# Moving ten of nineteen adaLN chunks of a two-layer trunk from TensorE matmuls to VectorE dot products

## The chip, the cores and the metric

The kernel runs on 1 core of one Trainium2 chip. The metric is the device time of one execution in microseconds (us). The time before is 1082.05 us, the median of 3 runs (1081.66 to 1082.13).

## The reference

Two layers work on 256 tokens of width 1024 in f32. Each layer first forms six modulation vectors of 1024 numbers from one conditioning vector (adaLN), then runs three attention branches between one input projection and one output projection, then a mixture of 16 experts.

```python
c_act = jax.nn.silu(c)
for layer in range(DEPTH):
    mod = jnp.dot(c_act, w_mod[layer]) + b_mod[layer]
    sh1, sc1, g1, sh2, sc2, g2 = jnp.split(mod[:, None, :], 6, axis=-1)
    u = rms_norm(x, norm1_g[layer]) * (1.0 + sc1) + sh1
    x = x + g1 * token_mixers(u, ...)      # w_in, 3 branches, gates, w_out
    u = rms_norm(x, norm2_g[layer]) * (1.0 + sc2) + sh2
    x = x + g2 * grouped_moe(u, ...)
return rms_norm(x, final_g)
```

What matters here is `mod`: a vector of 1024 times a 1024 x 6144 matrix, 24 MB of weights a layer, for a result of 6144 numbers.

## The kernel before

Tokens and channels stand on the 128 partitions. The program of each engine is one fixed order, written out by hand (`tc.manual_schedule()`); engines meet through semaphores.

**Stages.** The prologue is followed by the mixers of layer 0 (to about 320 us), its experts (to about 545 us), the mixers of layer 1 (to about 830 us) and its experts. A mixer is a list of 24 steps, two (`h` = 0, 1) for each of the twelve column groups in `ORDER`. A step multiplies the normalised tokens by one 1 MB block of `w_in` (48 or 24 matmuls), and `step_done` then runs, in the order of `INNER = 'FVTS'`, what is due: follow-ups, the values, the turn (transposes) and the scores of the attention jobs. The nine jobs start at steps 12 to 20 (`JOBS`). After the list come the branch projections, two gate projections `gA0` and `gA1` with the branch A in between, and the output projection.

**Splitting.** f32 weights are cut in two parts before TensorE reads them: `prep_one` casts half a block on ScalarE (line 279, high part) and subtracts it on VectorE (line 280, low part); `split_to` lets this run two halves ahead (`AHEAD`). Four buffers hold the halves.

**A job.** `act("S", step)` calls `scores` (line 692, TensorE), `softmax` (maxima on VectorE, lines 748 to 755; exponentials on ScalarE, line 758) and `normalise` (reciprocals on VectorE, line 767, which need the sums that the exponentials leave).

**The adaLN chunks.** A layer has 12 chunks of 512 numbers. `mod_matmul` (line 423) makes one with two 1 MB blocks and matmuls that use 32 columns of the array each; `mod_copy` (line 430, ScalarE) takes it out of PSUM; one step later `mod_finish` turns it with four transposes (line 437), reduces it on VectorE (line 439) and adds the bias (line 460, sometimes also 463). `MOD_PLAN` says at which step which (layer, chunk) is made: 13 chunks in the mixers of layer 0 (eight of its own, five of layer 1) and 6 in those of layer 1; `EDGE` puts one more between the experts of layer 0. The first four chunks of layer 0 are made otherwise, by `mod_rows` (line 450): the same weights, transposed, stand as rows of 1024 numbers, and one VectorE instruction multiplies such a block of 128 rows with the conditioning vector (`crow`) and adds up each row. A chunk is four blocks, in two units of `modt`.

**The stream.** All weights come through one list (`self.stream`, `plan`), issued by `pump` on the SP queue in that order, one DMA of 1 MB a unit, as soon as a slot is free: `raw0` to `raw5` (`RAW_BUFS`), and at times `x0` to `x4`, `h0` to `h3`, `uh`, `ul`, `gb`. A slot is freed when its reader is done, and the release pumps. The experts read 96 blocks of 1 MB in each layer through the same list; in the middle of them stands a branch that would do the experts' overflow (`rest`, line 1544) and isn't taken, and that TensorE, ScalarE and VectorE each pass.

Of the kernel before, what the change touches and what calls it, by code (L numbers as in the profile page):

```python
# [10 lines left out]
F32 = mybir.dt.float32  # L11
# [13 lines left out]
L = 2  # L25
D = 1024
T = 256
# [59 lines left out]
ONCES = ["gb"]  # L87

ORDER = ['gB0', 'gB1', 'bi', 'bq', 'cq', 'ck', 'cv', 'aq', 'ak', 'gC0', 'av', 'gC1']
RAW_BUFS = 6  # L90
LATE = ["x0", "x1", "x2"]
HALVES = ["h0", "h1", "h2", "h3"]
NEAR = 8


MOD_PLAN = [{5: (0, 4), 6: (0, 5), 7: (0, 6), 9: (0, 7), 11: (0, 8), 13: (0, 9), 14: (0, 10), 15: (0, 11), 17: (1, 0), 18: (1, 1), 19: (1, 2), 21: (1, 3), 22: (1, 4)}, {3: (1, 6), 5: (1, 7), 7: (1, 11), 8: (1, 10), 9: (1, 9), 14: (1, 8)}]
EDGE = {0: (1, 5)}
EDGE_AT = 7

# [51 lines left out]


class Unit:
    __slots__ = ("src", "n", "key", "tile", "slot", "halves", "block", "halved", "rows", "rest", "layer", "wide", "once")

    def __init__(self, key, src, n=512, block=None):
        self.key, self.src, self.n, self.block = key, src, n, block
        self.tile, self.slot, self.halves, self.halved = None, None, None, False
        self.rows, self.rest, self.layer, self.wide = False, None, 0, True
        self.once = False  # L160


class Kernel:
    def __init__(self, ctx, tc, a):
# [5 lines left out]
        self.stream, self.issued = [], 0  # L170
        self.slots = [f"raw{i}" for i in range(RAW_BUFS)]
        self.parts = list(HALVES)
# [21 lines left out]
    def t(self, pool, shape, dt, tag, bufs=1):  # L194
        return pool.tile(shape, dt, tag=tag, name=self.nm(tag), bufs=bufs)
# [9 lines left out]
    def pump(self):  # L205
        while self.issued < len(self.stream):
            u = self.stream[self.issued]
            if u.block is not None and u.block not in self.ready:
                return
            if u.rest is not None:  # L210
                self.load(u.rest, u.rest.src(), 1)
                self.issued += 1
                continue
            fits = [x for x in self.slots if u.layer <= self.l or x[0] == "r"]
            if u.once:
                fits = self.once + fits
            if not fits:
                return
            u.slot = fits[0]
            (self.once if u.slot in self.once else self.slots).remove(u.slot)  # L220
            if u.slot in ONCE:
                pool = {"gb": self.e}.get(u.slot, self.ring)
                u.tile = self.t(pool, [128, 4, 512], F32, u.slot, ONCE[u.slot])
            else:
                pool = {"uh": self.g, "ul": self.g}.get(u.slot, self.ring)
                u.tile = self.t(pool, [128, 4, 512], F32, u.slot)
            src = u.src()
            if u.rows:
                for b in range(2):
                    self.nc.sync.dma_start(u.tile[:, 2 * b:2 * b + 2], src[:, b])  # L230
            elif u.halved:
                for h in range(2 if u.halved == 2 else 1):
                    self.load(u, src, h)
            else:
                self.nc.sync.dma_start(u.tile[:, :, :u.n], src)
            self.issued += 1
# [104 lines left out]

    def cact_row(self):

        self.crow = self.t(self.w, [128, 2, 4, T], F32, "y")[:, 0].rearrange("p a b -> p (a b)")
        self.nc.sync.dma_start(self.crow[0:1], self.a["crow"])

    def fill_row(self):
# [336 lines left out]
    def scores(self, qt, q, blocks, k, kblock):  # L684

        nc = self.nc
        nk = 256 if qt else 128
        s = [self.psum("y") for _ in range(2)]
        for j, b in enumerate(blocks):
            for r in range(2):  # L690
                rows = slice(64 * r, 64 * r + 64)
                nc.tensor.matmul(s[r][:, nk * j:nk * j + nk], q[rows, b, 128 * qt:128 * qt + 128],
                                 k[rows, kblock(b), 0:nk], start=True, stop=True)
        return s
# [185 lines left out]
    def mixers(self, l, parts, angles):  # L880
        nc, a = self.nc, self.a
# [63 lines left out]
        state = {}  # L945

        jobs = {}

        def job(br, qt, blocks, s0):
            jobs[s0] = br, qt, blocks  # L950

        def scores(br, qt, blocks):
            q = {"A": lambda: self.qA, "B": lambda: self.qB, "C": lambda: self.qC}[br]()
            k = {"A": lambda: self.kA, "B": lambda: self.qkB, "C": lambda: self.kC}[br]()
            s = self.scores(qt, q, blocks, k, (lambda b: 0) if br == "B" else (lambda b: b))
            return self.softmax(br, qt, blocks, s)

        def act(what, step):
            if what == "F":
                for fn in after.get(step, ()):  # L960
                    fn()
            elif what == "V" and step - 3 in jobs:
                self.values(*jobs[step - 3], state.pop(step - 3))
            elif what == "T" and step - 2 in jobs:
                state[step - 2] = self.turn(jobs[step - 2][0], state[step - 2])
            elif what == "S" and step in jobs:
                state[step] = self.normalise(*jobs[step], *scores(*jobs[step]))

        def load_bias():
            self.bias = t(self.ring, [128, 8, T], F32, LATE[0])  # L970
# [27 lines left out]

        mods = MOD_PLAN[l]

# [8 lines left out]
        def step_done(step, c, h):  # L1009
            if h == 1:  # L1010
                post(c)
            for what in INNER:
                act(what, step)
            if step - 1 in mods:
                self.mod_finish(*mods[step - 1], held.pop("mod"))
            if step in mods:
                held["mod"] = self.mod_copy(self.mod_matmul(*mods[step]))
# [51 lines left out]
        self.router_shift()  # L1069
        for c in ("gA0", "gA1"):  # L1070
            outs = [self.psum("mm") for _ in range(2)]
            for _ in self.by_channel(("in", l, c), outs, *self.u_parts()):
                pass
            if c == "gA1":
                self.slots += ["uh", "ul"]
                self.pump()
            if c == "gA0":
                self.sg["A"] = t(w, [128, KT, T], F32, "sg", 2)
            for d in range(2):
                k = 4 * int(c[2]) + 2 * d  # L1080
                nc.scalar.activation(self.sg["A"][:, k:k + 2], outs[d].rearrange("p (e t) -> p e t", e=2), AF.Sigmoid)
            if c == "gA0":
                self.mh = [t(w, [128, 4, T], F32R, "q", 2) for _ in range(2)]
                self.ml = [t(w, [128, 4, T], F32R, "p", 2) for _ in range(2)]
            else:
                self.table(AF.Sqrt)
            self.branch("A", int(c[2]), False, True)
# [9 lines left out]
        for oc in range(2):  # L1097
            outs = [self.psum("mm") for _ in range(2)]
# [517 lines left out]
    def plan(self):  # L1616

        a = self.a

        def block(name, l, c, h, n=512):  # L1620

            o = sum(COLS[x][1] for x in list(COLS)[:list(COLS).index(c)]) * D if isinstance(c, str) else 1024 * 512 * c
            o += 512 * n * h
            return lambda: a[name][l, o:o + 512 * n].rearrange("(p k n) -> p k n", p=128, k=4)

        def mod(l, c):
            for h in range(2):
                self.add(("mod", l, c, h), block("w_mod", l, c, h), split=False)

        def rows(l, i):  # L1630
            u = self.add(("modt", l, i), lambda: a["w_modt"][l, 2 * i:2 * i + 2].rearrange("b p (a k) -> p b a k", a=2),
                         split=False)
            u.rows = True
            return u

        def fill(l, s):
            if s in MOD_PLAN[l]:
                mod(*MOD_PLAN[l][s])

        def proj(l, c):  # L1640
            n = COLS[c][1]
            for h in range(2):
                self.add(("in", l, c, h), block("w_in", l, c, h, n), n)

        for l in range(L):
            order = list(enumerate(half_order(l)))
            first = len(self.stream)
            if l == 0:
                for s in range(4):
                    rows(0, s).halved = 2  # L1650
                    rows(0, 4 + s).halved = 2
                    for i, c in enumerate(ORDER[:N_SPLIT]):
                        n = COLS[c][1]
                        key = ("in", l, c, s // 2)
                        if s % 2 == 0:
                            u = Unit(key, block("w_in", l, c, s // 2, n), n)
                            u.halved = 1
                            self.stream.append(u)
                        else:
                            u = Unit(("rest", *key), None)  # L1660
                            u.rest = next(x for x in self.stream if x.key == key)
                            self.stream.append(u)
                            u = u.rest
# [5 lines left out]
            for s, (c, h) in order:  # L1669
                n = COLS[c][1]  # L1670
                u = self.add(("in", l, c, h), block("w_in", l, c, h, n), n, split=l == 0 or s >= 2 * N_EDGE)
# [8 lines left out]
                    self.add(("br", l, br.upper(), c), block("w_branch_" + br, l, 0, c))  # L1680
            for c in range(2):
                proj(l, f"gA{c}")
                self.add(("br", l, "A", c), block("w_branch_a", l, 0, c))
            for oc in range(2):
                for h in range(2):
# [14 lines left out]
            for u in self.stream[-2:]:  # L1700
                u.halved, u.wide = 1, False
                r = Unit(("rest", *u.key), None)
# [116 lines left out]
```

## Time and profile before

| what | us |
|---|---|
| median of 3 runs | 1082.05 |
| the profiled execution | 1081.17 |
| its span | 1079.6 |
| TensorE busy in the span | 1040.0 |
| VectorE busy | 553.1 |
| ScalarE busy | 394.4 |
| bytes by DMA | 336.58 MB, mean 312 GB/s |

The span runs from the first to the last instruction; the execution is 1.6 us longer than its span. Busy time of TensorE counts modelled ends of pipelined matmuls, so the distance from one matmul's start to the next says more of its pace than a duration.

### The profile page before, as it was taken

The numbers are of one execution on the slowest core, as the hardware profiler recorded it, in microseconds if no ns is written. First come the engines' busy times: TensorE is split into PE (matmuls) and PEld (weight loads), VectorE is DVE, ScalarE is ACT, GpSimd is POOL, SyncE is SP. The second block draws the span as 40 slices with busy tenths as digits, with TensorE's granted clock in tenths as the row PEclk, the third lists the DMA queues.
The fourth block names the chain that finished last, engine by engine and source line by source line (L and its number), as shares of the span: only waits on it lengthen the run. The fifth ranks groups of instructions, "written<-read, shape, count | busy, mean of one in ns | idle before, by whom it ended". The sixth has DMA issues, their size and how long they took to land. (4 is left out here: it accounts for less than half of the span.)

```text
span 1079.6 us, 19208 instructions
## 1 busy us (share of the span) xinstructions
PE 1040.0 (96%) x7750; PEld 707.6 (66%) x7750; DVE 553.1 (51%) x1333; ACT 394.4 (37%) x746; POOL 1.5 (0%) x11
## 2 busy tenths in 40 slices
PE   7899999999999999999999999999998999979996
PEld 5778777799975444444388787779997534325344
DVE  6967767556643232222265687776664323222224
ACT  4445456664531111111144446777453211001021
POOL 0000000000000000000000000000000000000000
PEclk9999999999999999999999999999999999999997
DMA  9997776597676999999977966246765699999991
GB/s 348 341 360 305 301 290 239 216 369 269 234 304 227 383 420 420 418 420 421 407 284 284 345 259 234 80 157 245 266 236 229 250 390 420 421 418 419 421 381 39
DMA packets 53846, 336.58 MB, mean 312 GB/s; under 512 B 5617, under 2 KB 11889, under 8 KB 15474
## 3 DMA queue, kind: packets, MB, share of 16 engines
q1 hardware_dynamic: 53746, 335.25, 79.1%
q8 instruction: 63, 1.03, 0.4%
q14 instruction: 37, 0.30, 0.1%
HBM read 334.18 MB, written 1.05 MB: 311 GB/s over the span
## 5 line engine op out<-in xcount | busy, mean ns | idle before, releaser
L280 DVE TENSOR_TENSOR h<-raw,h 128x1024 fp32r<-128x1024 f32 (+1 forms) x130 | 152.5, 1214 | 59.7 <-ACT h L279 59.7
L1447 PE MATMUL mm<-raw,gb 128*32 128x512 f32 (+1 forms) x656 | 171.1, 596 | 1.2 <-DMA raw<-in_exp_w_dram 1.2
L612 PE MATMUL mm<-uh,h 128*128 128x256 f32 x480 | 138.7, 289 | 4.6 <-ACT h L279 4.6
L615 PE MATMUL mm<-uh,h 128*128 128x256 f32 x480 | 137.0, 285 | 2.7 <-DVE h L280 2.7
L614 PE MATMUL mm<-ul,h 128*128 128x256 f32 x480 | 136.3, 284 | 0.0
L279 ACT CAST h<-raw 128x1024 fp32r<-128x1024 f32 (+1 forms) x130 | 129.1, 1042 | 17.3 <-PE mm L869 7.2
L1527 DVE TENSOR_TENSOR x<-y,x 128x512 fp32r<-128x512 f32 (+1 forms) x34 | 22.5, 660 | 158.5 <-ACT x L1526 158.5
L612 PEld LDWEIGHTS mm<-uh,h 128*128 128x128 f32 x480 | 91.7, 191 | 14.5 <-issue 7.9
L1447 PE MATMUL mm<-x,gb 128*32 128x512 f32 (+1 forms) x312 | 94.5, 595 | 0.0
L615 PEld LDWEIGHTS mm<-uh,h 128*128 128x128 f32 x480 | 91.7, 191 | 3.8 <-DVE h L280 3.8
L614 PEld LDWEIGHTS mm<-ul,h 128*128 128x128 f32 x480 | 91.8, 191 | 0.0
L1413 DVE SCALAR_TENSOR_TENSOR xT<-y,mod,xT 128x256 f32<-128x256 f32 x128 | 53.3, 477 | 73.7 <-PE y L1538 73.7
L1447 PE MATMUL mm<-h,gb 128*32 128x512 f32 (+1 forms) x496 | 83.5, 595 | 0.0
L1447 PE MATMUL y<-raw,gt 128*32 128x512 f32 (+1 forms) x224 | 74.9, 594 | 0.0
L593 PE MATMUL mm<-h,uh 128*128 128x512 f32 (+1 forms) x176 | 71.1, 404 | 0.0
L595 PE MATMUL mm<-h,ul 128*128 128x512 f32 (+1 forms) x176 | 69.1, 393 | 0.0
L594 PE MATMUL mm<-h,uh 128*128 128x512 f32 (+1 forms) x176 | 69.0, 392 | 0.0
L1447 PEld LDWEIGHTS mm<-raw,gb 128*32 128x32 f32 (+1 forms) x656 | 44.1, 117 | 31.3 <-issue 26.6
L1357 ACT ACTIVATE gb<-y,mod,sc 128x256 f32<-128x256 f32 (+1 forms) x40 | 20.9, 522 | 100.0 <-DVE gb L1359 100.0
L1421 ACT COPY gt<-t 128x512 f32<-128x512 f32 x16 | 9.4, 586 | 128.0 <-PE t L1420 128.0
L1447 PE MATMUL y<-h,gt 128*32 128x512 f32 (+2 forms) x312 | 53.8, 572 | 1.4 <-ACT gt L1421 1.4
L1447 PEld LDWEIGHTS mm<-x,gb 128*32 128x32 f32 (+1 forms) x312 | 25.1, 122 | 43.3 <-issue 39.5
(319 smaller groups left out, 2059.5 us busy)
## 6 DMA issues: line engine op xcount, KB each, us to landing
raw<-in_exp_w_dram SPq DMA_DIRECT2D x78, 1024.0 KB, 14.8
raw<-in_w_in_dram SPq DMA_DIRECT2D x48, 1024.0 KB, 7.0
x<-in_exp_w_dram SPq DMA_DIRECT2D x45, 1024.0 KB, 15.5
h<-in_exp_w_dram SPq DMA_DIRECT2D x41, 1024.0 KB, 16.8
raw<-in_w_mod_dram SPq DMA_DIRECT2D x37, 1024.0 KB, 7.3
ul<-in_exp_w_dram SPq DMA_DIRECT2D x13, 1024.0 KB, 14.2
uh<-in_exp_w_dram SPq DMA_DIRECT2D x9, 1024.0 KB, 17.7
raw<-in_w_modt_dram SPq DMA_DIRECT2D x16, 512.0 KB, 7.3
```

Source lines behind the costliest of these rows:

```text
L279: nc.scalar.copy(hi[:, :, :u.n], src)
L280: nc.vector.tensor_sub(lo[:, :, :u.n], src, hi[:, :, :u.n].bitcast(F32))
L593: nc.tensor.matmul(o, uh, hi[:, k, :u.n], start=(kk == 0), stop=False)
L594: nc.tensor.matmul(o, uh, lo[:, k, :u.n], start=False, stop=False)
L595: nc.tensor.matmul(o, ul, hi[:, k, :u.n], start=False, stop=(kk == 7))
L612: nc.tensor.matmul(o, hi[:, k, cs], mh[kk], start=(kk == 0 and b % 2 == 0), stop=False, skip_group_check=True)
L614: nc.tensor.matmul(o, hi[:, k, cs], ml[kk], start=False, stop=False, skip_group_check=True)
L615: nc.tensor.matmul(o, lo[:, k, cs], mh[kk], start=False, stop=(kk == 7), skip_group_check=True)
L1357: self.nc.scalar.activation(out, src, AF.Identity, bias=shift, scale=scale)
L1413: nc.vector.scalar_tensor_tensor(self.xT[:, k + b], ps[:, T * b:T * b + T], self.mod[l][:, 5, k + b:k + b + 1], self.xT[:, k + b], op0=ALU ...
L1447: self.nc.tensor.matmul(o[c:c + step], lhs[:, c:c + step], x, start=start, stop=stop, skip_group_check=True)
L1527: self.nc.vector.tensor_sub(yl, ps, yh.bitcast(F32))
```

## The change

Five of the 13 chunks in the mixers of layer 0 and five of the 6 in those of layer 1 are no longer matmuls but `mod_rows`. In each layer three of them (six units, twelve blocks) stand in the attention steps 12 to 20, one or two blocks a step as `ROWS_IN` says, between `softmax` and `normalise`; the other two (four units of two blocks) stand in the loops over `gA0` and `gA1`, one unit after each `h`. The remaining matmul chunks move to other steps. A unit of `modt` is now stored with its two blocks side by side (8 KB a partition) and loaded by one DMA; the first eight units keep two DMAs of 512 KB. There are seven `raw` slots in place of six; `crow` has a place of its own for the whole kernel (before, it lay in a tile that the mixers wrote later), and the buffer `dynamic_dma_scratch_size` is set to 4 KB.

```diff
-RAW_BUFS = 6
+RAW_BUFS = 7
-MOD_PLAN = [{5: (0, 4), 6: (0, 5), 7: (0, 6), 9: (0, 7), 11: (0, 8), 13: (0, 9), 14: (0, 10), 15: (0, 11), 17: (1, 0), 18: (1, 1), 19: (1, 2), 21: (1, 3), 22: (1, 4)}, {3: (1, 6), 5: (1, 7), 7: (1, 11), 8: (1, 10), 9: (1, 9), 14: (1, 8)}]
+MOD_PLAN = [{5: (0, 7), 8: (0, 8), 11: (0, 9), 14: (0, 10), 16: (0, 11), 18: (1, 2), 20: (1, 3), 22: (1, 4)}, {9: (1, 9)}]
+ROWS_PLAN = [[(0, i) for i in range(8, 14)], [(1, i) for i in range(12, 18)]]
+ROWS_AT = (11, 12, 14, 15, 17, 18)
+ROWS_IN = {12: 1, 13: 1, 14: 2, 15: 1, 16: 1, 17: 2, 18: 1, 19: 1, 20: 2}
+ROWS_LATE = [[(1, i) for i in range(4)], [(1, i) for i in range(20, 24)]]
...
-        self.crow = self.t(self.w, [128, 2, 4, T], F32, "y")[:, 0].rearrange("p a b -> p (a b)")
+        self.crow = self.t(self.g, [128, D], F32, "crow")
...
+        blocks = iter([(i, b) for i in ROWS_PLAN[l] for b in range(2)])
...
             elif what == "S" and step in jobs:
-                state[step] = self.normalise(*jobs[step], *scores(*jobs[step]))
+                parts = scores(*jobs[step])
+                for _ in range(ROWS_IN[step]):
+                    i, b = next(blocks)
+                    self.mod_rows(*i, (b,))
+                state[step] = self.normalise(*jobs[step], *parts)
...
-            for _ in self.by_channel(("in", l, c), outs, *self.u_parts()):
-                pass
+            for h, _ in enumerate(self.by_channel(("in", l, c), outs, *self.u_parts())):
+                self.mod_rows(*ROWS_LATE[l][2 * int(c[2]) + h])
...
             if s in MOD_PLAN[l]:
                 mod(*MOD_PLAN[l][s])
+            if s in ROWS_AT:
+                rows(*ROWS_PLAN[l][ROWS_AT.index(s)])
...
                 proj(l, f"gA{c}")
+                for r in ROWS_LATE[l][2 * c:2 * c + 2]:
+                    rows(*r)
                 self.add(("br", l, "A", c), block("w_branch_a", l, 0, c))
...
-    nc = bacc.Bacc("TRN2", target_bir_lowering=False, num_devices=1)
+    nc = bacc.Bacc("TRN2", target_bir_lowering=False, num_devices=1, dynamic_dma_scratch_size=4096)
```

## Rows read from the trace of the kernel before

**Rows 1.** The page's part 1: busy time of each engine over the whole span.
```profile
PE 1040.0 (96%) x7750; PEld 707.6 (66%) x7750; DVE 553.1 (51%) x1333; ACT 394.4 (37%) x746; POOL 1.5 (0%) x11
```
**Rows 2.** Windows by stage: stretch, length, busy (instructions) of PE, PEld, DVE, ACT, POOL; clock; DMA.
```profile
53.00:320.00 267.00, 264.35 (x2019) 220.58 (x2022) 174.33 (x400) 143.43 (x279) 0.00 (x0) 1.00 0.75 290
556.00:830.00 274.00, 270.62 (x2054) 238.32 (x2054) 185.83 (x397) 149.25 (x282) 0.00 (x0) 1.00 0.63 234
330.00:545.00 215.00, 212.01 (x1590) 88.95 (x1589) 60.06 (x158) 30.52 (x54) 0.00 (x0) 1.00 0.97 397
```
**Rows 3.** TensorE's waits over the whole span: total us, times, longest.
```profile
PE y L1348 <- DVEq L1544: 6.9, 2, 5.9
...
PE mm L615 <- DVE h L280: 4.2, 6, 0.8
```
**Rows 4.** Timeline of TensorE, layer 0: a chunk's transposes, then another's matmuls, each with its successor.
```profile
159.92 0.66 PE L437 MATMUL t<-ident,modsb 128*128 128x128 f32 x4
160.34 0.48 PE L593 MATMUL mm<-h,uh 128*128 128x512 f32 x1
...
169.23 1.92 PE L423 MATMUL mm<-raw,cact 128*32 128x512 f32 x16
171.09 0.39 PE L612 MATMUL mm<-uh,h 128*128 128x256 f32 x1
```
**Rows 5.** Answers by source line for lines 450 and 439; timeline row of line 460.
```profile
L450 DVE SCALAR_TENSOR_TENSOR raw<-raw,y x16: 1217/1219/1226, 8.5 to 49.0; 128x1024 f32<-128x1024 f32 x16
...
L439 DVE TENSOR_REDUCE mod<-t x20: 104/167/175, 71.8 to 678.2; 128x4 f32<-128x16 f32 x20
...
10.91 0.16 DVE L460 TENSOR_TENSOR mod<-mod,sm 128x2 f32<-128x2 f32 x1
```
**Rows 6.** VectorE in the attention steps, layer 0: waits before 330 us, then timeline.
```profile
DVE rs L767 <- ACT p L758: 13.9, 9, 2.3
...
122.79 0.18 DVE L767 RECIPROCAL rs<-sums 128x4 f32<-128x4 f32 x1 [1.27 <-ACT p L758]
140.94 0.20 DVE L767 RECIPROCAL rs<-sums 128x8 f32<-128x8 f32 x1 [2.28 <-ACT p L758]
154.13 2.36 DVE L280 TENSOR_TENSOR h<-raw,h 128x1024 fp32r<-128x1024 f32 x2
```
**Rows 7.** Timeline of VectorE beside the gate projections of layer 0.
```profile
267.50 2.36 DVE L280 TENSOR_TENSOR h<-raw,h 128x1024 fp32r<-128x1024 f32 x2 [4.95 <-ACT h L279]
...
286.15 2.36 DVE L280 TENSOR_TENSOR h<-raw,h 128x1024 fp32r<-128x1024 f32 x2 [5.99 <-ACT h L279]
```
**Rows 8.** Layer 1, 616 to 700 us: VectorE's waits; then timeline rows of ScalarE and TensorE.
```profile
DVE sc L714 <- ACT p L708: 6.3, 2, 4.4
DVE p L753 <- PE y L692: 1.4, 2, 0.9
...
694.61 0.40 ACT L758 ACTIVATE p<-p,nmx 128x128 f32<-128x128 f32 x1 [3.88 <-DVE nmx L755]
...
700.23 1.14 PE L792 MATMUL t<-ident,p 128*128 128x128 f32 x8 [1.35 <-ACT x L656]
```
**Rows 9.** Experts, layer 0: last half block's issue and landing, its first reader; weight loads' DMA waits, whole span.
```profile
L242 SPq DMA_DIRECT2D ul<-in_exp_w_dram x1: 1547/1547/1547, 533.7 to 533.7; - x1
...
DMA to landing us min/median/max: 9.6/9.6/9.6
...
545.68 0.43 PE L1447 MATMUL y<-ul,gt 128*64 128x256 f32 x1
...
PEld mm L1447 <- DMA raw<-in_exp_w_dram: 3.0, 2, 1.6
```
**Rows 10.** TensorE behind the branch of line 1544 in layer 0 and layer 1; the window behind it.
```profile
455.88 0.47 PE L1348 MATMUL y<-oh,th 128*128 128x256 f32 x2 [1.05 <-DVEq L1544]
...
970.96 0.77 PE L1348 MATMUL y<-oh,th 128*128 128x256 f32 x2 [5.88 <-DVEq L1544]
...
969.10:975.90 6.80, 4.95 (x23) 4.98 (x24) 1.09 (x2) 1.13 (x2) 0.00 (x0) 0.50 1.01 418
```

More of the change, by code (lines that the diff above doesn't have):

```diff
@@ L153 @@
 class Unit:
-    __slots__ = ("src", "n", "key", "tile", "slot", "halves", "block", "halved", "rows", "rest", "layer", "wide", "once")
+    __slots__ = ("src", "n", "key", "tile", "slot", "halves", "block", "halved", "rest", "layer", "wide", "once")
     def __init__(self, key, src, n=512, block=None):
@@ L158, in __init__ @@
         self.tile, self.slot, self.halves, self.halved = None, None, None, False
-        self.rows, self.rest, self.layer, self.wide = False, None, 0, True
+        self.rest, self.layer, self.wide = None, 0, True
         self.once = False
@@ L227, in pump @@
             src = u.src()
[L228 to L231, printed above, removed]
+            if u.halved:
                 for h in range(2 if u.halved == 2 else 1):
@@ L1630, in rows @@
         def rows(l, i):
[L1631 to L1634, printed above, removed]
+            return self.add(("modt", l, i), lambda: a["w_modt"][l, i].rearrange("p b (a k) -> p (b a) k", a=2), split=False)
         def fill(l, s):
@@ L1789 @@
         "crow": f["c"],
-        "w_modt": f["w_mod"].transpose(0, 2, 1).reshape(L, 48, 128, D),
+        "w_modt": f["w_mod"].transpose(0, 2, 1).reshape(L, 24, 2, 128, D).transpose(0, 1, 3, 2, 4),
         "positions": f["positions"].reshape(2, 128).T,
```

## The prediction

> **What bounds the kernel now.** I read the page's totals first, then windows by stage, then who waits for whom, and at last timelines around the places that the diff touches. TensorE is busy in 96% of the span, VectorE in half of it [rows 1]. By stage nothing changes in that: in either mixer TensorE is busy for all but 2.7 us (layer 0) and 3.4 us (layer 1) of the stretch, at full granted clock, while the DMA engines are used to 0.75 and 0.63 and VectorE to about two thirds [rows 2]. In the experts of layer 0 TensorE is busy in 212 of 215 us and the DMA engines to 0.97: two limits lie close together there. TensorE's waits are few. The longest is one of 5.9 us behind the branch in the experts (of 6.9 in all), and for the low halves of weights from VectorE it loses 4.2 us in six waits [rows 3]. So from about 53 us on, time that TensorE doesn't have to spend is time won, as long as the halves still come in time and the experts' stream keeps up.
>
> **What is removed.** Ten chunks of matmuls. A chunk's 16 matmuls start at 169.23 and their successor at 171.09: 1.86 us. Four transposes start at 159.92, the next matmul at 160.34: 0.42 us [rows 4]. Together 2.28 us a chunk, 22.8 us for ten, half in each layer. With each chunk go a copy on ScalarE, which TensorE doesn't wait for, and on VectorE a reduction of 0.17 us and a bias addition of 0.16 us [rows 5]. The chunks that stay as matmuls are only moved to other steps, at the same price.
>
> **What is added.** Forty VectorE instructions of 1.22 us, and two bias additions a chunk in place of one [rows 5]: 49 us on an engine that isn't the bound. Some cover is needed all the same, because VectorE works in order and the low halves stand behind the dot products.
>
> Twelve blocks a layer stand between a job's maxima and its reciprocals. There VectorE already waits for the exponentials: 13.9 us in nine waits a layer, about 1.27 us in a job of four exponentials and 2.28 us in one of eight [rows 6]. One block (1.22) fills the short wait, two blocks (2.44) the long one, so only the biases and the third job's excess run over: some 0.2 to 0.4 us in six of the nine steps, 2 us a layer together. The exponentials don't wait for the dot products, only the reciprocals do. In layer 0 I cost this at nothing: the halves that end at 156.49 (154.13 + 2.36) are first read at 160.34 [rows 4, 6], a cover of 3.9 us, and steps there lie alike.
>
> The trace has no such dot product beside an exponential; the 16 in it stand alone. The bounds are 0, if all fits the waits, and 12 x 1.22 = 14.6 us a layer if the wait only moves behind it. I take 0 for layer 0 and the next paragraph's term for layer 1, because the wait is for ScalarE, which the block doesn't use.
>
> [...] By the row a block of 1024 numbers takes 1.22 us. [...]
>
> **Layer 1 gives some back.** There VectorE is almost without idle time from the first top-k (617 us) to 700 us. What waits it has for TensorE are the second of 6.3 us in two (6.3 - 4.4 = 1.9) and 1.4 for scores [rows 8]; the rest are ScalarE's exponentials. TensorE already stands at 700.23 for 1.35 us for a copy of ScalarE, which stands behind exponentials that waited 3.88 us for VectorE's maxima [rows 8]. After the scores of step 8 TensorE loses two chunks' work, less pieces that lie before it: about 5.2 us. VectorE can move forward by its own waits (1.9 + 1.4 = 3.3), gains 1 us of reductions and biases, and pays about 0.9 us of overrun in the steps before: 3.4 us. So 5.2 - 3.4 = 1.8 us of the gain stays in a wait near 700 us. Bounds: 0, and 5.2 if VectorE can't move at all.
>
> **The late units.** Beside `gA0` and `gA1` four units of 2.44 us and biases stand in each layer: VectorE idles there for 4.95 us before 267.50 and 5.99 us before 286.15 [rows 7], each time enough for two. I cost them at nothing; without that cover they would cost up to 9.8 us a layer.
>
> **Transfers.** Bytes and DMAs stay, but four units a layer now stand behind `gA0` and `gA1`, ahead of the expert weights, on the one SP queue; each release by VectorE holds up what is behind it there only until a block is done. The experts' stream is the risk: in layer 0 the last half block is issued at 533.7, lands 9.6 us later at 543.3, and is first read at 545.68, so 2.4 us are to spare [rows 9]. In the late mixer the DMA engines have idle time, and the units' slots come back before the output projection ends, so the fill at the experts' start is the same, plus one block for the seventh slot. That block also takes away most of the 3.0 us that weight loads wait for DMA at the start of the two expert stages [rows 9]; I take 2. Bounds: 0, and 3. The 4 KB buffer is used by no transfer that the page shows, so it costs nothing.
>
> **The sum.** -22.8 - 2 + 1.8 = -23.0 us. Against the profiled execution's 1081.17 that is 1058.2; the median stands 0.9 us higher, so I forecast 1059. Its own range, by the bounds of layer 1 (0 to 5.2), of DMA (0 to 3) and 2 us for overruns in layer 0, is 1056 to 1066.
>
> **Rivals.** (a) The branch. Behind it TensorE stands 5.88 us in layer 1 and 1.05 us in layer 0 for the same instruction of VectorE, and in layer 1 the granted clock is then at the lower of its two levels for 6.8 us, in which TensorE is busy for 4.95 us, half of it lost [rows 10]. That is 5.88 - 1.05 + 2.5, some 7 us by chance of place, as nothing in the work differs. VectorE's code gets longer by some 50 instructions a layer, so the place changes. If layer 1 passes as layer 0 did, the time is 1059 - 7 = 1052. If layer 0 stands as well, 1066. [...]
>
> (b) The cover is short: VectorE holds the low halves up through layer 1, where it has no idle time. If half of the twelve blocks' time (7.3 us) and half of the late ones' (4.9 us) comes through there, the time is 1059 + 12 = 1071. For it: VectorE's continuous work in [rows 8]. Against it: the waits of [rows 6, 7] are as long as the blocks.
>
> (c) Slower: VectorE waits for a unit that hasn't landed, and the halves wait behind it. It needs more than 23 us, over 20 units 1.2 us each; at 1.5 us it gives 1059 + 30 = 1089. Against it: every unit stands in the list ahead of weights that TensorE needs in the same or the next step, and TensorE waits for weights by DMA only in the experts [rows 9].
>
> (d) The matmuls that go were hidden, so nothing moves: 1082. It needs TensorE to wait elsewhere for as long; its 2.7 and 3.4 us of idle time in the mixers [rows 2] say it doesn't.
>
> **How the numbers follow.** The forecast has 0.50. Of rival (a), 1052 gets 0.25 and 1066 gets 0.11, less than the other since layer 0 must get worse while layer 1 stays. (b) has 0.09, (c) 0.03, (d) 0.02. The range 1050 to 1068 takes in the forecast with its bounds and both cases of (a), and leaves out (b) to (d) and the tail of 1052 with several favours at once. About 2 us (0.2%) is what a measurement can tell from no change: faster 0.95, same 0.02, slower 0.03.
>
> **What would show it.** Right: line 423 with 16 x 9 matmuls in the mixers in place of 16 x 19; line 450 with 56 instructions of 1.22 us; the waits of line 767 nearly gone; no new wait of TensorE for line 280 in layer 0 and a longer one near the 700.23 row in layer 1; each mixer shorter by 9 to 12 us. Wrong: TensorE waiting for low halves in several steps (b), VectorE waiting for `modt` (c), or expert weight loads waiting for DMA at the end of layer 0, where only 2.4 us are to spare. A wait behind the branch of another length than 1.05 and 5.88 us is rival (a).

## The result and the profile after

The kernel after takes 1067.96 us (median of 4 runs, 1065.12 to 1068.17) against 1081.86 for the kernel before (4 runs beside them): ratio 0.9863, 95% interval 0.985 to 0.9875. The forecast was 1059, the range 1050 to 1068: the median lies inside by 0.04 us, and one of the four runs (1068.17) outside. The profiled execution took 1067.82 us, its span 1066.0. Lines of the kernel after lie 3 to 9 behind those of before (450 is 453, 767 is 770, 1544 is 1552).

Part 1 of the page after, against [rows 1]:

```profile
PE 1018.6 (96%) x7550; PEld 703.6 (66%) x7550; DVE 598.0 (56%) x1414; ACT 388.8 (36%) x736; POOL 1.5 (0%) x11
```

TensorE does 200 matmuls and 21.4 us less, VectorE 44.9 us more. Windows by stage, against [rows 2] (same columns; mixers of layer 0, of layer 1):

```profile
53.00:308.50 255.50, 252.84 (x1918) 217.84 (x1922) 196.70 (x440) 140.54 (x273) 0.00 (x0) 0.99 0.79 305
552.50:816.60 264.10, 259.13 (x1957) 234.77 (x1957) 208.75 (x439) 147.08 (x278) 0.00 (x0) 1.00 0.64 239
```

Both mixers are shorter, and TensorE still does little but work in them. Where the rest went is in TensorE's waits over the span, against [rows 3]:

```profile
PE y L1356 <- DVEq L1552: 11.8, 2, 6.0
...
PE mm L618 <- DVE h L283: 4.2, 6, 0.8
...
PE mm L1455 <- DMA raw<-in_exp_w_dram: 1.6, 2, 0.9
```

The waits for low halves are the same to the tenth. The wait behind the branch has grown from 6.9 to 11.8 us: layer 0 now stands as layer 1 did. (Below, a branch *stands* when VectorE waits at it for some 5.6 us, and *passes* when it goes on after 0.8 us.) Timeline rows of TensorE behind the two branches, against [rows 10]:

```profile
449.35 0.76 PE L1356 MATMUL y<-oh,th 128*128 128x256 f32 x2 [5.95 <-DVEq L1552]
...
957.48 0.77 PE L1356 MATMUL y<-oh,th 128*128 128x256 f32 x2 [5.89 <-DVEq L1552]
```

The window behind the one of layer 0, also against [rows 10], at a granted clock of 0.50 (the traces of before and after have stretches at 1.00 and at 0.50 and at nothing between; *the lower clock* below is 0.50):

```profile
447.80:454.60 6.80, 5.25 (x24) 5.28 (x25) 1.09 (x2) 1.13 (x2) 0.00 (x0) 0.50 1.01 419
```

To say what each stage gave, I cut the span at starts of TensorE that every kernel has: its first matmul of an adaLN chunk (62.47 us before, 63.79 after), the first matmuls on the router's mask (line 1218 before), the first gather behind the branch, the first sums of squares of layer 1. The lengths, in us, for all kernels of this study (e1 to e12 are below):

| kernel | mixers 0 | experts 0 to branch | behind it | mixers 1 | experts 1 to branch | behind it |
|---|---|---|---|---|---|---|
| before | 260.6 | 132.8 | 97.6 | 280.3 | 137.2 | 108.6 |
| after | 247.7 | 137.9 | 101.4 | 269.7 | 137.1 | 108.5 |
| e4, before, both branches pass | 260.6 | 132.7 | 98.9 | 280.6 | 132.3 | 105.9 |
| e3, after, both pass | 247.7 | 132.8 | 98.9 | 270.2 | 132.3 | 105.7 |
| e5, e3 with 6 slots | 248.1 | 137.8 | 97.6 | 270.4 | 137.3 | 105.2 |
| e12, e4 with 7 slots | 260.5 | 130.9 | 99.4 | 280.1 | 130.5 | 105.3 |
| e6, attention part, dense | 262.2 | 131.0 | 97.7 | 274.8 | 132.1 | 105.2 |
| e11, attention part, spread | 252.8 | 131.0 | 98.2 | 273.8 | 132.1 | 105.2 |
| e7, late part | 256.6 | 132.7 | 98.7 | 275.9 | 133.8 | 105.7 |
| e8, e3 without the cover | 258.8 | 132.9 | 99.5 | 281.7 | 133.9 | 106.4 |

From before to after: mixers -12.9 and -10.6, experts of layer 0 +5.1 and +3.8, experts of layer 1 -0.2, the start +1.3: -13.5 of the span. The column "behind it" of layer 0 moves by 1.3 us between profiles without a cause in the kernel (e4 only shifts the code of layer 1): the lower clock at the layers' border lasts 3.4 us in some (before) and 6.8 in others (after). The start moves likewise: in the profile after, a stretch of 3.4 us at the lower clock begins at 55.3 us, in the one before at 44.1. The kernel before was run again beside each batch of experiments, with medians from 1080.92 to 1082.28 us, so medians of different batches compare only to about 1.4 us; e3, e4 and e5 are of one batch.

### The profile page after: what moved, and what is told of

Same layout as the page of the kernel before. It is cut to its first block, busy times and chain, and to the rows that moved or that the text cites. A ratio compares the mean times of both kernels' runs of the same rounds, so it can differ in the third digit from the quotient of the medians.

```text
span 1066.0 us, 18867 instructions
## 1 busy us (share of the span) xinstructions
PE 1018.6 (96%) x7550; PEld 703.6 (66%) x7550; DVE 598.0 (56%) x1414; ACT 388.8 (36%) x736; POOL 1.5 (0%) x11
## 5 line engine op out<-in xcount | busy, mean ns | idle before, releaser
L283 DVE TENSOR_TENSOR h<-raw,h 128x1024 fp32r<-128x1024 f32 (+1 forms) x132 | 154.7, 1213 | 32.0 <-ACT h L282 31.9
L1455 PE MATMUL mm<-raw,gb 128*32 128x512 f32 (+1 forms) x640 | 160.9, 596 | 1.6 <-DMA raw<-in_exp_w_dram 1.6
L618 PE MATMUL mm<-uh,h 128*128 128x256 f32 x480 | 137.3, 286 | 2.7 <-DVE h L283 2.7
L282 ACT CAST h<-raw 128x1024 fp32r<-128x1024 f32 (+1 forms) x132 | 131.0, 1041 | 20.2 <-PE mm L618 9.8
L1455 PE MATMUL mm<-h,gb 128*32 128x512 f32 (+1 forms) x376 | 101.4, 595 | 0.0
L615 PEld LDWEIGHTS mm<-uh,h 128*128 128x128 f32 x480 | 92.1, 192 | 11.8 <-ACT h L282 7.5
L1455 PE MATMUL y<-raw,gt 128*32 128x512 f32 (+2 forms) x424 | 89.4, 570 | 1.4 <-ACT gt L1429 1.4
L1455 PEld LDWEIGHTS mm<-raw,gb 128*32 128x32 f32 (+1 forms) x640 | 41.1, 116 | 56.1 <-issue 49.9
L1455 PE MATMUL y<-x,gt 128*32 128x512 f32 (+2 forms) x232 | 64.7, 580 | 0.7 <-ACT gt L1429 0.7
L453 DVE SCALAR_TENSOR_TENSOR raw<-raw,crow 128x1024 f32<-128x1024 f32 x52 | 62.0, 1219 | 1.0 <-ACT uv L480 1.0
## 6 DMA issues: line engine op xcount, KB each, us to landing
raw<-in_exp_w_dram SPq DMA_DIRECT2D x77, 1024.0 KB, 15.5
uh<-in_exp_w_dram SPq DMA_DIRECT2D x12, 1024.0 KB, 15.8
```

The lines of the kernel that those rows point to most:

```text
L282: nc.scalar.copy(hi[:, :, :u.n], src)
L283: nc.vector.tensor_sub(lo[:, :, :u.n], src, hi[:, :, :u.n].bitcast(F32))
L453: nc.vector.scalar_tensor_tensor(v[:, b], v[:, b], 1.0, self.crow, op0=ALU.mult, op1=ALU.mult, accum_out=self.mod[l][:, j, k0 + b:k0 + b + 1])
L615: nc.tensor.matmul(o, hi[:, k, cs], mh[kk], start=(kk == 0 and b % 2 == 0), stop=False, skip_group_check=True)
L618: nc.tensor.matmul(o, lo[:, k, cs], mh[kk], start=False, stop=(kk == 7), skip_group_check=True)
L1455: self.nc.tensor.matmul(o[c:c + step], lhs[:, c:c + step], x, start=start, stop=stop, skip_group_check=True)
```

## The experiments

**What lets a branch pass.** VectorE's branch, its going on (the semaphore instruction behind the branch) and the notice of the branch that `mark_branch_hint_location` gives it earlier, by line in the kernel after:

```profile
L1822 DVEq BRANCH_PREFETCH_HINT  x2: 50/56/61, 436.5 to 944.5; - x2
...
L1552 DVEq COMPARE_BRANCH  x2: 78/81/84, 443.5 to 951.7; - x2
...
L1552 DVEq EVENT_SEMAPHORE  x2: 21/21/21, 449.2 to 957.3; - x2
```

The same for the branch before:

```profile
L1544 DVEq COMPARE_BRANCH  x2: 78/81/84, 454.9 to 965.2; - x2
L1544 DVEq EVENT_SEMAPHORE  x2: 21/21/21, 455.7 to 970.8; - x2
```

The columns are count, duration in ns, first and last start. VectorE itself stands 5.7 and 5.6 us at its branch; before it was 0.8 (454.9 to 455.7) in layer 0 and 5.6 in layer 1, with the same 7 us from notice to branch each time. TensorE waits for VectorE, not for its own branch, which is behind it at 443.5 in layer 0 of the kernel after. Nor does ScalarE's matter: it stands 5.0 to 5.6 us in both layers of every profile here, the fastest included.

So I moved code. The expectations speak of places: a place is the number of VectorE instructions that lie ahead in the built program, those that never run included, modulo 256 in e1 and e2 and modulo 128 later. In e1 and e2 I moved code by instructions that never run, at the end of the branch's body:

```diff
+            for _ in range((236, 186)[l]):      # e2, in the kernel before: (0, 209)
+                nc.vector.memset(cw[:, 0, 0:1], 0.0)
```

> The kernel after, with 236 and 186 VectorE instructions put at the end of the two branch bodies, which never run. Counted in the built program, the place where VectorE goes on behind the branch moves to 41 modulo 256 in both layers (61 and 131 in the kernel after; 41 and 88 in the one before, of which only the 41 passed in 0.8 us); the branches themselves stay at 182 and move from 252 to 232. Theory A, the place of the branch's target decides: VectorE resumes some 0.8 us behind its branch in both layers, TensorE waits about 1 us instead of 5.9 us in each, the lower clock behind it goes, 7 us a layer: 1068 - 14 = 1054. Theory B, the place of the branch itself decides (162 passed; 182, 209 and 252 did not): both still stand, 1068. Theory C, the expert stream takes over in layer 0 where the DMA engines are used to 0.98: both waits go, but half of the 7 us of layer 0 comes back as weight loads waiting for DMA, 1057 to 1061.

> The kernel before, with 209 VectorE instructions that never run at the end of layer 1's branch body: the target of layer 1 moves from 88 to 41 modulo 256, the branch stays at 209; layer 0 keeps 162 and 41. Theory A, the place of the target decides: layer 1 passes like layer 0, about 7 us less, 1082 - 7 = 1075. Theory B, the place of the branch decides: nothing moves, 1082.

e1 took 1059.18 us (ratio 0.9797, 0.9774 to 0.982): layer 1 passed (948.2 to 949.0), layer 0 stood (442.0 to 447.6). e2 took 1082.41 (1.0005, 0.9994 to 1.0016): layer 1 stood. Neither A nor B holds as written: targets at 41 stood twice, and layer 1 of e1 passed where B had it stand. C was not tested, as layer 0 stood. Only the traces then showed that VectorE runs more instructions than I had counted (a dot product is two, the second a `DVE_READ_ACCUMULATOR` of 0.08 us, and so is each `MATCH_REPLACE8` of the top-k, with a `MATCH_VALUE_LOAD` of 0.09 us ahead of it), so the counts were put right, and modulo 128 sorted all cases by the place of the notice: 54 and 55 passed, 75, 94 and 120 stood. The next two kernels test that. e3 gives VectorE's notice alone earlier, by 42 VectorE instructions in layer 0 and 18 in layer 1, and leaves the branches where they are; e4 is the kernel before with never-run instructions as in e1, `(62, 0)[l]` of them:

```diff
+HINT_AT = (("M2", 2), ("L0", 1))
-            if (what, name, x) == ("in", GROUPS[REST_AT - 1][-1], IN_STEPS - 2):
+            if (what, name, x) == ("in", *HINT_AT[l]):
                 self.beyond = self.nc.values_load(self.more[0:1], min_val=0, max_val=32 * T + 32)
-                self.tc.mark_branch_hint_location(f"rest{l}", self.beyond, (PE, DVE, ACT))
+                self.tc.mark_branch_hint_location(f"rest{l}", self.beyond, (DVE,))
+            if (what, name, x) == ("in", GROUPS[REST_AT - 1][-1], IN_STEPS - 2):
+                self.tc.mark_branch_hint_location(f"rest{l}", self.beyond, (PE, ACT))
```

> [...] Counted with the extra instructions that the traces show, and modulo 128 (the instruction fetches of VectorE's queue in the trace are of 8 KB), the notices stood at 54 in the two cases that passed in 0.8 us and at 75, 94 and 120 in those that stood for 5.6 us; here they stand at 52 and 57. Theory A, the place of the notice decides: both branches pass, TensorE waits about 1 us in each, 1068 - 15 = 1053, or 1055 to 1058 if the expert stream of layer 0 takes part of it back as weight loads waiting for DMA. Theory B, the place of the branch decides (67 passed; 5, 88 and 107 stood): both still stand, 1068. Theory C, neither, only chance from run to run: no forecast, and the two layers need not agree.

> The kernel before, with 62 VectorE instructions that never run at the end of layer 0's branch body, which moves everything of layer 1: notice and branch there to 54 and 67 modulo 128, as in layer 0. If the place of notice or branch decides: TensorE's wait behind the branch of layer 1 falls from 5.9 to 1 us and the lower clock behind it goes, 1082 - 8 = 1074. If not: 1082. With e3_hint_early it gives the change's own worth without the branch: my steps say 23 us between the two (22.8 for the chunks, 2 for the slot, less 1.8 in layer 1).

e3 took 1051.56 us (0.9727, 0.9711 to 0.9743), e4 1074.68 (0.9941, 0.9925 to 0.9958). Both branches pass in both. TensorE's waits in e3 and then in e4, for the branch and for expert weights:

```profile
PE y L1357 <- DVEq L1553: 2.1, 2, 1.0
...
PE mm L1456 <- DMA raw<-in_exp_w_dram: 1.5, 2, 0.8
...
PE y L1348 <- DVEq L1544: 2.1, 2, 1.0
...
PE mm L1447 <- DMA raw<-in_exp_w_dram: 1.4, 2, 0.7
```

And e3's timeline rows behind the two branches:

```profile
443.00 0.48 PE L1357 MATMUL y<-oh,th 128*128 128x256 f32 x2 [1.05 <-DVEq L1553]
...
944.38 0.48 PE L1357 MATMUL y<-oh,th 128*128 128x256 f32 x2 [1.05 <-DVEq L1553]
```

By the table a branch that stands costs 7.6 us more than one that passes: e3 against after in the experts of layer 1 (132.3 + 105.7 against 137.1 + 108.5), e4 against before in the same place, e3 against after in layer 0. The price isn't a constant: layer 0 of e1, which stood, took 137.6 and 98.9 us, 6.1 more than that of the kernel before. There the lower clock began at 444.0 us, 3.8 us ahead of the end of the wait, and TensorE was busy for only 2.99 us of it; in the kernel after for 5.25 us. The stream of layer 0 takes nothing of it back. Was it the place or the lead, which e3 made longer too?

```diff
-HINT_AT = (("M2", 2), ("L0", 1))
+HINT_AT = (("L0", 1), ("L0", 1))
+            for _ in range((19, 0)[l]):
+                nc.vector.memset(cw[:, 0, 0:1], 0.0)
```

> Was it the place of the notice or its lead that let e3_hint_early pass? There the notices came 60 and 43 us ahead of the branch at places 52 and 57; in e1_place_after layer 1 passed with 7 us of lead at 55. Here VectorE's notice comes early in both layers, about 45 us ahead, but at place 76 (in layer 1 with 19 never-run VectorE instructions in layer 0's body), next to the 75 at which layer 1 of the kernel after stood. Place decides: both branches stand for 5.6 us, TensorE waits 11.8 us in two, time about 1068. Lead decides: both pass, about 1052.

One run, 1066.14 us, and both stood, 43 us after their notices:

```profile
L1553 DVEq COMPARE_BRANCH  x2: 78/81/84, 441.9 to 950.2; - x2
L1553 DVEq EVENT_SEMAPHORE  x2: 21/21/21, 447.5 to 955.7; - x2
```

So the place of the notice decides, and not its lead. Over all 14 profiles here, 51 to 57 passed in every case (21), 75, 76, 94 and 120 stood in every case (7), wherever branch and target lay: in e3 both branches lie where they do in the kernel after. Where the borders are, and why, was not tried.

**The slot.**

```diff
-RAW_BUFS = 7        # e5, from e3
+RAW_BUFS = 6
```

> As e3_hint_early, with six raw slots in place of seven; the places of notices and branches are the same to one instruction. My step said that the seventh slot saves 2 us of weight loads waiting for DMA at the experts' starts (bounds 0 and 3): then this one is 2 us slower than e3_hint_early, with the wait of line 1455 for DMA at about 3 us in place of 1. The rival: the trace of the kernel after still has 1.6 us of that wait in two, so the slot is worth nothing there, 0 us. A third: VectorE or ScalarE wait for units with six slots, since four rows units stand in the list at the late projections, 3 us and more.

e5 took 1060.46 us, 8.9 more than e3: more than my bounds, and not the rival either. TensorE's wait for expert weights in e5:

```profile
PE mm L1456 <- DMA raw<-in_exp_w_dram: 8.2, 2, 4.1
```

The window behind the first of the two waits:

```profile
334.50:337.90 3.40, 3.40 (x20) 0.85 (x16) 0.00 (x0) 0.00 (x0) 0.00 (x0) 0.51 0.26 108
```

At each experts' start TensorE stands 4.1 us for a block and then works 3.4 us at the lower clock (0.51 in the window): 5 us a layer in the table. e12 puts the slot into e4, with the other memory edits of the change:

```diff
-RAW_BUFS = 6
+RAW_BUFS = 7
-        self.crow = self.t(self.w, [128, 2, 4, T], F32, "y")[:, 0].rearrange("p a b -> p (a b)")
+        self.crow = self.t(self.g, [128, D], F32, "crow")
-    nc = bacc.Bacc("TRN2", target_bir_lowering=False, num_devices=1)
+    nc = bacc.Bacc("TRN2", target_bir_lowering=False, num_devices=1, dynamic_dma_scratch_size=4096)
```

> The kernel before with the notices at the passing place (e4_before_both, 1074.7) and only the memory part of the change: seven raw slots, the conditioning row in a place of its own, the 4 KB buffer; all chunks stay matmuls. My step: the slot saves 2 us of weight loads waiting for DMA at the experts' starts (bounds 0 and 3): 1072.7. What the runs since then suggest: those waits are about 1.4 us in all in the kernel before with six slots and stay so with seven, so nothing is won, 1074.7; the slot is worth 8.9 us only together with the late units (e5_six_slots).

1070.79 us, 3.9 less than e4 (another batch); the wait for expert weights is gone from TensorE's waits, 1.7 and 1.8 us at the two starts (132.7 to 130.9, 132.3 to 130.5). So the slot, with the other memory edits, is worth about 3.5 by the table, and the late units take it back. The lists of DMA issues show how, with the first expert matmul at 0: e4 has issued 18 expert blocks by then and the next at 3.7 us; e12 19, the next at 3.7; e3 19, but the next at 7.1; e5 18 and the next at 7.1, in both layers. With the late units in the list the next slot comes free a block later.

**The two parts.** e6 has the dot products of the attention steps alone, e7 the late ones alone, the other chunks as matmuls; the notices stand at passing places.

```diff
-MOD_PLAN = [{..., 14: (0, 10), 16: (0, 11), 18: (1, 2), 20: (1, 3), 22: (1, 4)}, {9: (1, 9)}]
+MOD_PLAN = [{..., 14: (0, 10), 16: (0, 11), 17: (1, 0), 18: (1, 1), 19: (1, 2), 21: (1, 3), 22: (1, 4)}, {7: (1, 11), 8: (1, 10), 9: (1, 9)}]   # e6, ROWS_LATE empty
+MOD_PLAN = [{5: (0, 4), 6: (0, 5), 7: (0, 6), 9: (0, 7), 11: (0, 8), 13: (0, 9), 14: (0, 10), 15: (0, 11), 18: (1, 2), 20: (1, 3), 22: (1, 4)}, {3: (1, 6), 5: (1, 7), 9: (1, 9), 14: (1, 8)}]   # e7, ROWS_PLAN empty
```

> The attention part alone: three chunks a layer as dot products in the attention steps, the other four of the change as matmuls (layer 1's 0 and 1 at steps 17 and 18 of layer 0, its 11 and 10 at steps 7 and 8 of layer 1); seven slots; the notices of the branch at the place that passes in both layers, as in e3_hint_early, so the frame is e4_before_both (1074.7: nothing moved) and e3_hint_early (1051.6: both parts). My steps: six chunks of 2.28 us are 13.7, less 1.8 that layer 1 gives back: 1074.7 - 11.9 = 1062.8, and 1060.8 if the seventh slot saves its 2 us. If the dot products were not covered at all, 12 blocks of 1.22 us a layer would come back in layer 1: 1077.

> The late part alone: four chunks as dot products beside the two late gate projections of both layers, nothing in the attention steps; seven slots; notices at the place that passes. My steps: four chunks of 2.28 us, cost nothing: 1074.7 - 9.1 = 1065.6. If the late units delay the experts' stream even with seven slots, the wait of line 1455 for DMA grows from 1.5 us and the time with it: above 1067. The parts should add up: (1074.7 - e6) + (1074.7 - e7) = 23.1; more or less than that by over 2 us would be an interaction.

e6 took 1065.94 us, e7 1067.65: 8.7 and 7.0 below e4, together 15.8 of 23.1. e7's forecast was 1065.6; its wait for expert weights didn't grow (1.3 us), but the start of layer 1's experts is 1.5 us longer than in e4, with 3.4 us at the lower clock at the router. What is missing from the sum is in the mixers of layer 0 of e6, 1.6 us longer than e4's. Timeline rows of TensorE there:

```profile
172.16 0.66 PE L659 MATMUL t<-ident,rope 128*128 128x128 f32 x4 [2.30 <-DVE mod L443]
...
177.82 1.97 PE L796 MATMUL t<-ident,p 128*128 128x128 f32 x8 [3.55 <-ACT x L660]
```

And the window behind them:

```profile
173.30:183.50 10.20, 6.65 (x34) 4.24 (x34) 4.22 (x7) 5.04 (x10) 0.00 (x0) 0.50 0.98 388
```

Line 443 is the reduction of a chunk made with matmuls: four of them now stand in neighbouring steps (16 to 19) beside the jobs. The kernel before has three in a row (17 to 19) without such a wait, but no dot products there. e11 spreads them:

```diff
-MOD_PLAN = [{5: (0, 7), 8: (0, 8), 11: (0, 9), 14: (0, 10), 16: (0, 11), 17: (1, 0), 18: (1, 1), 19: (1, 2), 21: (1, 3), 22: (1, 4)}, ...]
+MOD_PLAN = [{5: (0, 7), 6: (0, 8), 8: (0, 9), 9: (0, 10), 11: (0, 11), 14: (1, 0), 16: (1, 1), 18: (1, 2), 20: (1, 3), 22: (1, 4)}, ...]
```

> As e6_attention, with layer 0's ten matmul chunks at other steps (5, 6, 8, 9, 11, 14, 16, 18, 20, 22 in place of 5, 8, 11, 14, 16, 17, 18, 19, 21, 22), so that no two stand in neighbouring steps beside the attention jobs. In e6_attention TensorE waited for VectorE's chunk reduction and a copy of ScalarE at 172 and 178 us of layer 0, with the clock at its lower level for 10 us behind it. If that is what my placing of the chunks cost: the waits go and the time is 1059 to 1061 (my steps: 1074.7 - 11.9 - 2 for the slot = 1060.8; what is left of e3's 23.1 beside e7's 7.0 is 16.1, which gives 1058.6). If the dot products themselves do it, the waits stay: 1066.

1058.02 us (0.9785, 0.9769 to 0.9802), 16.7 below e4; the two waits are down to 0.17 us in one. With e7's 7.0 the parts make 23.7, against 23.1 for both. e11 also keeps the slot's gain at the start of layer 0's experts, which e3 doesn't, so the mixers alone compare better: against e4 those of e11 are 14.5 us shorter and those of e7 8.7, together 23.2, as many as e3's 12.9 and 10.4. e9 is e6 with six slots:

```diff
-RAW_BUFS = 7
+RAW_BUFS = 6
```

> As e6_attention with six raw slots. e5_six_slots lost 8.9 us against e3_hint_early, at the experts' starts (weight loads waiting for DMA 4.1 us twice, and the lower clock behind it), where the kernel before with six slots waits 1.4 us in all. Theory A, the late units do it (they hold slots beside the last projections, so the experts' stream starts later): here, without late units, the wait stays near 1.5 us in all and the time equals e6_attention within 1 us. Theory B, the shorter mixers do it (less time to fetch ahead, whatever stands late): the wait is there too, 3 us or more in all, and the time is 3 to 6 us above e6_attention.

1076.54 us, 10.6 more than e6, but not where either theory had it: the experts' starts lose 1.9 and 2.3 us, and 5.0 more are lost in the crowded steps of layer 0 (TensorE waits 6.5 us for ScalarE at 183.5). As e6's plan was itself at fault, the time doesn't settle which theory holds. The wait speaks for A: TensorE waits for expert weights 1.9 us in three, near the 1.4 of e4 and far from e5's 8.2. With e12 and the issue times above that puts the price on the late units.

**The cover.** e8 is e3 with the dot products behind the job's reciprocals:

```diff
                 parts = scores(*jobs[step])
+                state[step] = self.normalise(*jobs[step], *parts)
                 for _ in range(ROWS_IN[step]):
                     i, b = next(blocks)
                     self.mod_rows(*i, (b,))
-                state[step] = self.normalise(*jobs[step], *parts)
```

> As e3_hint_early, with the dot products of the attention steps behind the job's reciprocals and not ahead of them. VectorE then waits for the exponentials first (9 waits, 13.9 us a layer, as before the change) and the blocks come on top, ahead of the low halves. My step says that the waits are the cover: without it up to 14.6 us a layer of VectorE's time come through where it has nothing to spare, layer 1 from 617 to 700 us, so 5 to 15 us slower than e3_hint_early there (1057 to 1067), and little in layer 0, where the halves are 3.9 us ahead. Rival: the place makes no difference, since TensorE's order already leaves the halves enough lead: 1052.

1072.2 us (1069.98 to 1077.62), 20.6 more than e3, and more than expected. The profiled execution is the slowest of the four, 5.4 us above the median: in it the mixers of layer 0 are 11.1 us longer than e3's, those of layer 1 11.5, so the cost by layer holds only roughly. VectorE's wait for the exponentials in layer 0 is back as in [rows 6]:

```profile
DVE rs L771 <- ACT p L762: 13.8, 9, 2.3
```

And TensorE waits in both layers, in layer 0 mostly for copies of ScalarE (timeline rows):

```profile
151.09 1.11 PE L659 MATMUL t<-ident,rope 128*128 128x128 f32 x4 [3.53 <-ACT q L660]
...
663.25 0.50 PE L598 MATMUL mm<-h,uh 128*128 128x512 f32 x1 [1.52 <-DVE h L284]
...
696.35 1.97 PE L796 MATMUL t<-ident,p 128*128 128x128 f32 x8 [2.70 <-ACT x L660]
```

## Why the prediction was right, and where it was not

The measured time lies at the very end of the range, and that it lies just inside is luck: 13.9 us were won where 23 were forecast. The range held because its upper end took in the case of rival (a) in which both branches stand.

The change without the branch is e4 to e3: 1074.68 to 1051.56, 23.1 us. The steps said 23.0; how close that is owes something to luck too, as the terms below show. From before to after layer 1's branch stands on both sides, and layer 0's newly costs 7.6 by the table: -23.1 + 7.6 = -15.5, where the medians differ by 13.9. The 1.6 between them is less than what the start and the layers' border moved in the profile after (1.3 each), which come and go between profiles.

**The step that failed** is the sum's silent term for the branch. It took the branches as they were, one passing and one standing. The cause and the price were in rival (a), "If layer 0 stands as well, 1066", but with 0.11, "less than the other since layer 0 must get worse while layer 1 stays". Nothing supported that order. Of the four places that the two kernels took without intent (54 and 120 before, 94 and 75 after) one passed, that of layer 0 before. This hints that code added ahead of it was likelier to lose it than to win layer 1, but doesn't show it: the places from 58 to 74, and most of the others, were not tried. The traces of before had the notice, 7 us ahead in both layers, and the two lengths; the prediction read only the lengths.

**Chunks removed.** 2.28 us each was a little low for layer 0: 12.9 for five is 2.57 (e11's three gave 7.7, also 2.57 each; e7's two 4.0, with a new wait of 1.2 us in that plan). The starts from which it was read leave out something at a chunk's ends; the runs don't name it.

**Dot products hidden.** Right. The durations beside exponentials are those that stood alone, and the reciprocals follow without a wait; the answer by source line for 453:

```profile
L453 DVE SCALAR_TENSOR_TENSOR raw<-raw,crow x52: 1215/1219/1226, 8.8 to 782.2; 128x1024 f32<-128x1024 f32 x52
```

And the timeline of two jobs of layer 0:

```profile
117.29 1.22 DVE L453 SCALAR_TENSOR_TENSOR raw<-raw,crow 128x1024 f32<-128x1024 f32 x1
118.44 0.08 DVE L453 DVE_READ_ACCUMULATOR raw<-raw,crow 128x1 f32 x1
118.65 0.18 DVE L770 RECIPROCAL rs<-sums 128x4 f32<-128x4 f32 x1
...
132.58 1.22 DVE L453 SCALAR_TENSOR_TENSOR raw<-raw,crow 128x1024 f32<-128x1024 f32 x1
133.72 0.08 DVE L453 DVE_READ_ACCUMULATOR raw<-raw,crow 128x1 f32 x1
133.72 1.22 DVE L453 SCALAR_TENSOR_TENSOR raw<-raw,crow 128x1024 f32<-128x1024 f32 x1
134.87 0.08 DVE L453 DVE_READ_ACCUMULATOR raw<-raw,crow 128x1 f32 x1
134.99 0.16 DVE L463 TENSOR_TENSOR mod<-mod,sm 128x2 f32<-128x2 f32 x1
135.06 0.20 DVE L770 RECIPROCAL rs<-sums 128x8 f32<-128x8 f32 x1
```

The price of a block held on all 56 instructions (the other four, on `x` slots, take 1218 to 1222 ns). My reason for 0 in layer 0, halves that are 3.9 us ahead, was not the one that mattered: e8 shows that without the waits as cover layer 0 loses some 11 us in the profiled execution, within the bounds but not nothing.

**Layer 1 gives some back.** Right in size, wrong in place. Five chunks at layer 0's 2.57 are 12.9; layer 1 won 10.4 (e4 to e3), so 2.5 stayed, where I had 1.8. By e7, whose two chunks gave 4.7 in layer 1 without a new wait, it is 1.4; the new wait shown below is 1.6. The 5.2 us of the prediction doesn't follow from its own price: two chunks at 2.28 are 4.6, and less pieces of them is less, so the term would have been 1.2 at most. The chain is the one described, but it bites two jobs earlier (timeline rows of ScalarE and TensorE in the kernel after, against [rows 8]):

```profile
662.41 0.51 ACT L761 ACTIVATE p<-p,nmx 128x256 f32<-128x256 f32 x1 [5.08 <-DVE nmx L758]
...
666.92 1.14 PE L795 MATMUL t<-ident,p 128*128 128x128 f32 x8 [1.57 <-ACT q L659]
...
687.20 1.14 PE L795 MATMUL t<-ident,p 128*128 128x128 f32 x8 [1.36 <-ACT x L659]
```

The row of 687.20 is the old one of 700.23, as long as before; the one of 666.92 is new, and e6 and e11 have it too.

**Late units.** On VectorE they cost nothing, as said: e7 gains 4.0 and 4.7 us in the mixers for two chunks each. As transfers they cost what the next step was to win: "the fill at the experts' start is the same" is wrong, since the next slot comes free at 7.1 in place of 3.7 us.

**Seventh slot.** The 2 us were about 3.5 by itself, above the bound of 3, and 0 in the change: the wait for expert weights stays at 1.5 us. Without it the change would have lost 8.9 (e5). In the sum this miss of 2 and the chunks' extra price cancel, which is luck.

**Rivals (b), (c), (d)** did not come: no new waits for low halves, none of VectorE for a unit, and the matmuls were not hidden. Nor did the end of layer 0's experts suffer: no matmul of e3 waits for weights there, though nothing stands at the branch any more.

## What to carry to other kernels

A branch whose body isn't run cost up to 7.6 us more or less here, by where the notice of it lies in VectorE's code, so a kernel with one should be compared with its branch passing on both sides, and one notice moved by some instructions is worth trying before any work is moved: here it is worth more than half of the change (e3, 1051.56 us, is the fastest kernel of the study). The long VectorE instructions (1.22 us) were free inside waits that were already there, as long as they are (1.27 and 2.28 us), and ahead of the instruction that waits; behind it (e8, 20.6 us more) they were not. The units put into the shared stream of loads had their price where the stream runs short (the next expert block issued at 7.1 us in place of 3.7), not where they are used.

## What was not expected of the hardware

In these runs the wait at the branch depended on the place of the notice and not on its lead: 7 us of lead were enough at 54 and 55, and 43 us were not at 76. The packets of a queue that the page calls instruction differ with it. The page's part 3 for the kernel after (queue, packets, MB, share):

```profile
q14 instruction: 38, 0.31, 0.1%
```

They are of 8 KB; the trace names no engine for them. In layer 0 of the kernel before one starts at 451.89, 3.9 us behind VectorE's notice at 448.04 and ahead of the branch at 454.94. In layer 0 of the kernel after none starts between 439.30, which lies 3.5 us behind ScalarE's own notice (as 450.92 does before), and VectorE's branch; one starts at 447.20, 3.7 us behind the branch at 443.51, and VectorE goes on at 449.18. In layer 0 of the kernel before, where VectorE goes on at 455.7, one starts 3.8 us behind the branch too (458.76). So the notice at the place that stood was not followed by such a packet ahead of the branch; why not, and what the packets bring, the traces don't show. The other profiles agree: in 20 of the 21 cases that passed such a packet starts 3.8 to 4.2 us behind VectorE's notice (18.8 in layer 0 of e7), and in none of the seven that stood does one start at that distance. VectorE waits some 5.6 us (5.5 to 5.7) at a branch that stands, and 0.8 where such a packet had followed the notice.

Long waits of TensorE went with 3.4 to 6.8 us of the lower clock: 6.8 at 0.50 with the 5.9 us at the branch ([rows 10]), 3.4 at 0.51 behind the 4.1 us for a block (e5). The 4.9 us that a standing branch adds to the wait cost 6.1 to 7.6 us by the table.
